# Idle-time products in the routing, a first expert step in two parts, and one leaf for its second block

## The chip, the cores and the metric

The kernel runs on one core of a Trainium2 chip. A core has TensorE (matrix products, written to PSUM), VectorE, ScalarE, GpSimd and SyncE, which run their own instruction streams and wait for each other by semaphores, and 16 DMA engines that move data between HBM and the on-chip memory SBUF. The metric is the device time of one execution in microseconds (us), lower is better; times of a kernel are given as the median of several runs.

## The reference

A decoder trunk of two layers over 256 tokens of 1024 numbers, in float32. Each layer: a mixer (gated MLP over chunks, differential attention, pooling), residual and layer norm, a feed-forward part, residual and layer norm. The feed-forward part of layer 0 is a dense SwiGLU; that of layer 1 sends each token to its two best of eight experts:

```python
logits = (xt @ router_w).astype(F32)
top_v, top_i = lax.top_k(logits, TOP_K)
top_w = jax.nn.softmax(top_v, axis=-1)
gates = jnp.sum(jax.nn.one_hot(top_i, N_EXPERTS, dtype=F32) * top_w[..., None], axis=1)
for e in range(N_EXPERTS):
    y = y + gates[:, e:e + 1].astype(x.dtype) * swiglu(xt, w1[e], w3[e], w2[e])
```

An expert has w1 and w3 of 1024 x 3584 and w2 of 3584 x 1024, so the eight of them are 352 MB, nearly all that the kernel reads.

## The kernel before

Layer 0, the second mixer and the routing come first; the experts take the last two thirds of the time.

**The weights' pieces.** All large weights are cut into pieces of 128 partitions x 1024 numbers (512 KB). The list `units` has them in the order of use, and `pump_loads` (L170) issues a piece's load on SyncE's queue as soon as a place is free. In the expert stage there are 34 places (10 + 8 + 16), and the piece m can be loaded when piece m - 34 has been given back: `place_of` (L155) compares with `state["done"]`, which `done(n)` raises. Places are given back in program order, and a load whose place was read within a branch waits until TensorE has passed that branch. Before the routing has ended, only the pieces whose address is known without it can be loaded; they fill the 34 places.

**The steps.** Each expert is worked through in seven steps of 512 of its 3584 columns. `order()` (L50) interleaves two lanes of experts into 56 steps; steps 0 to 5 and 7 belong to the expert in front of lane 1, called `first`, step 6 to the first one of lane 0. A step takes 4 pieces of w1, 4 of w3 and, but for an expert's first step, 4 of w2 (for the columns of the step before); its program is `step(mode)` in the loop at L1257: `h_part` (L1214) makes the products with w1 into `bank[0]` and with w3 into `bank[1]`, `y_part` (L1243) those with w2, and `turn` (L1225) transposes the result for the next step. After the step `done` gives its pieces back.

**Counts, blocks and leaves.** Which tokens an expert gets is known on the chip alone. `first` is always the weights' expert 0, whatever its count; the other seven are ranked by their count, and `MOST_OF` (L59) says how many tokens the expert of a rank can have at most: 256 for the ranks 0 to 2, 170 for rank 3, 128 and less behind it. Those above 128 have a second block of 128 tokens. `by_count` (L1157) writes each block's work several times, as leaves of an If: "full" for more than 64 tokens in the block, "pair" for 33 to 64 (two groups of 64 columns side by side), "quad" for up to 32 (four of 32). The second block's leaves stand within an If on a count over 128. All leaves are in the instruction stream, one behind another, and an engine jumps over those that are not taken; TensorE's are by far the longest, since each float32 product is two records with a weight load each.

**The routing.** `finish` (L872) is the end of the second mixer for the second 128 tokens: it normalises them, turns them (`turned`, L797), makes their logits (8 products with 8 columns) and chooses two experts per token (`choose`, L814). From `finish` on the instructions of every engine stand in the order in which they are written (`manual_schedule`). Then come the tokens' places within their expert (`pk`, L896 to L899), VectorE's copies of these, the clearing of the PSUM banks that the expert stage uses (L981), the selection matrix of the first expert (`gather_sel`, L1006), the count into registers (`load_count`, L987), the sort of the experts by count, and the gather of the first expert's tokens (`gather`, L1050), 16 products with a moving side of 64 columns. GpSimd scatters the tokens to HBM for the others.

## Time and profile before

| what | value |
|---|---|
| median of 3 runs | 1405.44 us (1399.57 to 1407.64) |
| the profiled execution | 1409.62 us, span 1407.9 us |
| TensorE busy (matmul) | 1254.7 us, 89% |
| VectorE, ScalarE, GpSimd busy | 412.7, 300.8, 103.0 us |
| mean granted clock of TensorE | 0.952 |
| DMA, mean over the span | 316 GB/s |

The span is the time from the program's first instruction to its last; the execution's own time is a little longer. [...] "Busy" of TensorE means that a product is under way. In rows of the timeline a bracket says how long the engine was idle before the row and what ended that; PEq or ACTq is the sequencer of TensorE or ScalarE, which jumps and issues, and "issue" means that nothing in the profile ended the wait.

### The profile page before, as it was taken

The page shows a single profiled execution, that of the slowest core. Times are in us where ns is not written, and L with a number is a line of the kernel's source. Part 1 is how long each engine was busy: PE and PEld are TensorE (multiplying, and loading weights), DVE is VectorE, ACT ScalarE, POOL GpSimd, SP SyncE. Part 2 cuts the span into 40 slices and gives each one's busy share as a digit, 9 for nine tenths or more (in the row PEclk, how much of TensorE's full clock was granted, in tenths as well). Part 3 has the DMA queues.
Part 4 walks back from the last instruction along what each step waited for, and adds up shares of the span by engine and source line. Part 5 has one row for each costly group of instructions (what it writes and reads, how often), then busy time and mean ns, then how long its engine had stood idle before and what let it go on. Part 6 is the DMA issues. An engine that isn't in the chain of part 4 may idle for free. (4 is left out here: it accounts for less than half of the span.)

```text
span 1407.9 us, 18436 instructions
## 1 busy us (share of the span) xinstructions
PE 1254.7 (89%) x6282; PEld 689.6 (49%) x6282; DVE 412.7 (29%) x674; ACT 300.8 (21%) x515; POOL 103.0 (7%) x162
## 2 busy tenths in 40 slices
PE   7989999999888778899989887988988999999875
PEld 6977888879863223334333332423433344433221
DVE  3757454566641111112121111111121021111123
ACT  3646444445520001110011000111110100001101
POOL 2111000010122000000000000000000000000161
PEclk9999999999987989999999999999999999999997
DMA  8995565564495997989999999799999999999995
GB/s 256 385 334 174 187 208 178 186 194 161 119 358 195 343 382 264 339 313 391 392 385 393 393 364 362 263 340 336 368 381 393 385 392 392 393 394 359 397 394 207
DMA packets 204428, 445.38 MB, mean 316 GB/s; under 512 B 14759, under 2 KB 36838, under 8 KB 204232
## 3 DMA queue, kind: packets, MB, share of 16 engines
q1 hardware_dynamic: 199192, 426.49, 83.2%
q0 software_dynamic: 5040, 16.20, 3.2%
q8 instruction: 133, 2.18, 0.6%
q14 instruction: 63, 0.52, 0.1%
HBM read 427.42 MB, written 15.21 MB: 314 GB/s over the span
## 5 line engine op out<-in xcount | busy, mean ns | idle before, releaser
L1182 PE MATMUL bank<-raw,xg 128*32 128x512 f32 (+2 forms) x2240 | 519.4, 639 | 82.9 <-issue 41.7
L1182 PEld LDWEIGHTS bank<-raw,xg 128*32 128x32 f32 (+2 forms) x2240 | 183.7, 141 | 374.1 <-issue 321.2
L1182 PE MATMUL py<-raw,gT 128*64 128x512 f32 (+2 forms) x880 | 226.0, 607 | 3.0 <-issue 1.4
L1223 DVE COPY hB<-bank 128x512 f32<-128x512 f32 x56 | 38.7, 692 | 462.1 <-PE bank L1182 434.6
L199 DVE TENSOR_TENSOR lo<-raw,hi 128x1024 fp32r<-128x1024 f32 x118 | 141.6, 1221 | 85.8 <-ACT hi L198 82.8
L1182 PEld LDWEIGHTS py<-raw,gT 128*64 128x64 f32 (+2 forms) x880 | 85.5, 144 | 132.0 <-issue 115.1
L198 ACT ACTIVATE hi<-raw 128x1024 fp32r<-128x1024 f32 x118 | 121.6, 1056 | 82.2 <-PE h L232 36.2
L1219 ACT ACTIVATE g<-bank 128x512 f32<-128x512 f32 x70 | 41.8, 597 | 339.7 <-PE bank L1182 339.7
L1237 DVE TENSOR_REDUCE gm<-bank 128x128 f32<-128x512 f32 (+1 forms) x112 | 74.1, 688 | 103.5 <-PE bank L1230 99.0
L1240 ACT ACTIVATE gm<-gm 128x128 f32<-128x128 f32 (+1 forms) x56 | 19.6, 350 | 318.1 <-DVE gm L1237 318.1
L232 PE MATMUL h<-hi,x1Th 128*128 128x512 f32 (+1 forms) x192 | 70.8, 375 | 0.8 <-DVE x1Tl L236 0.6
L1221 DVE TENSOR_TENSOR gm<-g,bank 128x512 f32<-128x512 f32 x14 | 9.6, 688 | 208.7 <-PE bank L1182 208.7
L232 PE MATMUL h<-hi,x1Tl 128*128 128x512 f32 (+1 forms) x192 | 70.4, 372 | 0.0
L232 PE MATMUL h<-lo,x1Th 128*128 128x512 f32 (+1 forms) x192 | 54.4, 372 | 0.0
L1037 POOL DMA_DIRECT2D stage<-far_rows x9 | 4.9, 540 | 594.0 <-PE bank L1063 427.5
L1230 PEld LDWEIGHTS bank<-ident,g 128*128 128x128 f32 x224 | 23.8, 142 | 48.4 <-issue 45.0
L1232 ACT ACTIVATE gT<-bank 128x512 f32<-128x512 f32 x14 | 8.4, 597 | 178.7 <-PE bank L1230 178.7
L232 PE MATMUL ph<-hi,mix 128*128 128x512 f32 x128 | 41.0, 397 | 0.0
L232 PEld LDWEIGHTS h<-hi,x1Th 128*128 128x128 f32 x192 | 36.1, 188 | 7.5 <-DVE x1Tl L236 1.0
L232 PEld LDWEIGHTS h<-hi,x1Tl 128*128 128x128 f32 x192 | 36.2, 188 | 6.5 <-DVE x1Tl L236 0.4
L1230 PE MATMUL bank<-ident,hB 128*128 128x128 f32 x224 | 34.9, 279 | 4.5 <-DVE hB L1223 2.3
L1230 PE MATMUL bank<-ident,g 128*128 128x128 f32 x224 | 36.9, 288 | 1.2
(335 smaller groups left out, 1233.3 us busy)
## 6 DMA issues: line engine op xcount, KB each, us to landing
raw<-in_moe_w_dram SPq DMA_DIRECT2D x672, 512.0 KB, 10.5
raw<-in_ffn_w_dram SPq DMA_DIRECT2D x66, 512.0 KB, 4.5
raw<-in_w_in_dram SPq DMA_DIRECT2D x36, 512.0 KB, 4.3
far_rows<-zeros SPq DMA_DIRECT2D x8, 1024.0 KB, 11.7
raw<-in_w_out_dram SPq DMA_DIRECT2D x16, 512.0 KB, 8.8
stage<-far_rows POOLq DMA_DIRECT2D x7, 256.0 KB, 7.8
lnp<-in_ln_g_dram POOLq DMA_DIRECT2D x6, 256.0 KB, 3.7
lnp<-in_ln_b_dram POOLq DMA_DIRECT2D x6, 256.0 KB, 5.6
```

Source lines behind the costliest of these rows:

```text
L198: A.activation(hi, t, AF.Copy)
L199: V.tensor_tensor(lo, t, f32(hi), op=ALU.subtract)
L232: T.matmul(o, st, mv, start=start and i == 0, stop=stop and i == len(pairs) - 1)
L1037: G.dma_start(out=stage[b_][0:w, :], in_=far_rows[r:r + w, :])
L1182: T.matmul(o[j * w:(j + 1) * w], x_(k, w), row[:, cols], start=first and k < parts, stop=last and k >= len(ws) - parts)
L1219: A.activation(gs[b_], o, AF.Silu if mode == "full" else AF.Copy)
L1221: V.tensor_tensor(gm, gs[b_], o, op=ALU.mult)
L1223: V.tensor_copy(hB[b_], o)
L1230: T.transpose(pt[:, c * P:(c + 1) * P], h[:, c * P:(c + 1) * P], ident)
L1232: A.activation(d, bank[2], AF.Copy)
L1237: V.tensor_reduce(t[:, 0:4 * w].rearrange("p (c t) -> p c t", c=4), pt.rearrange("p (c j t) -> p c t j", c=4, j=parts), axis=AX.X, op=ALU.add)
L1240: A.activation(t1, t1, AF.Silu)
```

## The change

There are three edits.

First, `keep_going` makes two products of the identity with rows of `xcur` into a PSUM tile that nobody reads. It is called in `finish` between the row scale and the turning of the tokens, once behind the mixer, and once behind the places `pk`. Its tile comes from the rotation of four banks from which the expert stage takes its own, so one of those is the same memory.

Second, the first expert's second block has one leaf, "full", in the gather and in `by_count`; a leaf for 128 tokens is right for fewer too.

Third, in step 0 the products with w1 are made for all blocks in a `by_count` of their own, the four pieces of w1 are given back, and then the step goes on with w3; `h_part` skips a weight with no pieces.

```diff
@@ finish
         row_scale(xs, nmu, sq, rs)
+        idle.append(rot("idle"))
+        keep_going()
         pl, lg = logits(turned(us))
...
-    lgs, lranks = [], []
+    lgs, lranks, idle = [], [], []
+
+    def keep_going():
+
+        for i in range(2):
+            T.matmul(idle[0], ident, xcur[:, 0, i * 512:(i + 1) * 512], start=True, stop=True)
+
     bias_logits()
     mixer(1, xT, lambda: transpose_x(xT, 1, 0, 8), route_0, bcast(ln1_g[1]), bcast(ln1_b[1]), finish)
+    keep_going()
     pk = acc("pslot")
...
+    keep_going()
     first = LANES[1][0]
@@ gather
-        if MOST_OF[e] > P:
+        if e == first:
+            with tc.If(n > P):
+                block(1, P)
+        elif MOST_OF[e] > P:
@@ by_count
-        if b_:
+        if b_ and e == first:
+
+            with tc.If(n > P):
+                go("full")
+        elif b_:
             with tc.If(n > P):
                 modes()
@@ h_part
         for o, ws in zip(bank, (w1, w3)):
+            if not ws:
+                continue
@@ the loop over the steps
         w2 = take(4) if i else []
+        if s == 0:
+
+            for b_ in blocks(e):
+                by_count(e, b_, lambda mode: h_part(q, b_, mode, w1, []))
+            w1 = []
+            done(4)
...
-        done(8 + len(w2))
+        done(len(w1) + 4 + len(w2))
```

## Rows read from the trace of the kernel before

**Rows 1.** Stretches: length, busy us (instructions) by engine, clock, DMA share, GB/s.
```profile
420.00:442.00 22.00, 17.92 (x72) 10.82 (x72) 5.04 (x19) 2.88 (x6) 9.27 (x26) 0.70 0.24 94
442.00:640.00 198.00, 164.04 (x733) 67.86 (x734) 28.50 (x47) 19.03 (x38) 3.27 (x6) 0.92 0.92 331
640.00:820.00 180.00, 164.49 (x756) 66.72 (x755) 30.29 (x50) 16.59 (x33) 2.17 (x4) 0.96 1.04 391
820.00:1030.00 210.00, 185.62 (x887) 73.65 (x889) 34.30 (x57) 23.34 (x47) 4.29 (x8) 0.95 0.92 337
```

**Rows 2.** Waits over the span: us in total, times, longest.
```profile
PE bank L1182 <- issue: 41.7, 18, 6.9
...
PEld bank L1182 <- DMA raw<-in_moe_w_dram: 32.4, 45, 4.4
...
PE bank L1182 <- PEq L1171: 23.8, 10, 3.8
```

**Rows 3.** Timeline of SyncE's queue from 440 us: start, us, instruction, count.
```profile
442.41 4.00 SPq L184 DMA_DIRECT2D raw<-in_moe_w_dram  x6
```

**Rows 4.** TensorE's timeline, first records of steps 1 to 6 and the gather.
```profile
443.00 8.78 PE L1182 MATMUL bank<-raw,xg 128*64 128x512 f32 x32 [3.68 <-PEq L1171]
...
461.28 8.42 PE L1182 MATMUL bank<-raw,xg 128*64 128x512 f32 x32 [5.04 <-issue]
...
477.49 8.78 PE L1182 MATMUL bank<-raw,xg 128*64 128x512 f32 x32 [3.34 <-PEq L1171]
...
494.58 8.78 PE L1182 MATMUL bank<-raw,xg 128*64 128x512 f32 x32 [3.84 <-PEq L1171]
...
514.75 8.99 PE L1182 MATMUL bank<-raw,xg 128*64 128x512 f32 x32 [6.92 <-issue]
...
531.37 2.14 PE L1063 MATMUL bank<-ident,stage 128*128 128x128 f32 x16 [3.18 <-PEq L1171]
533.44 16.79 PE L1182 MATMUL bank<-raw,xg 128*128 128x512 f32 x32
```

**Rows 5.** TensorE's timeline, later steps without a long gap in front.
```profile
557.82 7.09 PE L1182 MATMUL bank<-raw,xg 128*64 128x512 f32 x32 [0.31 <-ACT gm L1240]
...
570.79 0.93 PE L1063 MATMUL bank<-ident,stage 64*128 64x64 f32 x8 [1.42 <-ACTq L1171]
...
586.89 13.97 PE L1182 MATMUL bank<-raw,xg 128*128 128x512 f32 x32 [0.48 <-PEq L1171]
...
1206.86 7.09 PE L1182 MATMUL bank<-raw,xg 128*64 128x512 f32 x32
```

**Rows 6.** TensorE's timeline, steps behind steps of the expert of rank 3.
```profile
801.77 14.00 PE L1182 MATMUL bank<-raw,xg 128*128 128x512 f32 x32 [0.90 <-ACTq L1171]
...
863.72 8.58 PE L1182 MATMUL bank<-raw,xg 128*64 128x512 f32 x32 [5.20 <-issue]
...
879.80 15.67 PE L1182 MATMUL bank<-raw,xg 128*128 128x512 f32 x32 [3.03 <-PEq L1171]
```

**Rows 7.** Stretches of the routing and one step end; clock third from the right.
```profile
404.00:412.00 8.00, 5.79 (x37) 4.62 (x36) 4.46 (x19) 4.19 (x8) 0.67 (x2) 1.00 1.05 387
413.00:433.00 20.00, 15.01 (x58) 11.43 (x60) 6.51 (x38) 2.55 (x5) 12.85 (x46) 0.50 0.48 185
...
568.00:572.00 4.00, 2.54 (x20) 1.71 (x20) 1.71 (x3) 1.05 (x3) 0.00 (x0) 1.00 0.30 93
```

**Rows 8.** Timeline of all engines in the routing.
```profile
410.66 1.36 PE L803 MATMUL pxT<-ident,u 128*128 128x128 f32 x8 [2.10 <-DVE u L882]
...
411.97 2.86 PE L810 MATMUL plog<-rw,x1T 128*128 128x8 f32 x16
...
418.43 0.66 DVE L1018 TENSOR_SCALAR se<-misc,slot 128x256 f32<-128x256 f32 x2
```

**Rows 9.** TensorE's timeline, the first gather and step 0.
```profile
420.24 7.06 PE L1061 MATMUL bank<-se,xcur 128*128 128x64 f32 x32 [2.45 <-DVE hB L921]
428.10 9.64 PE L1182 MATMUL bank<-raw,xg 128*64 128x512 f32 x32 [0.80 <-POOL hB L947]
```

## The prediction

> **What bounds the kernel now.** I read the stretches first [rows 1]. Where the transfers never wait (640 to 820 us) their share is 1.04, so in another stretch they idle for its length times (1 - share/1.04): 16.9 us of 420 to 442, 22.8 us of 442 to 640, 24.2 us of 820 to 1030. The reader sees a kernel that moves expert weights as fast as it ever does for long stretches, and two places in which the transfers stand still. Then the waits [rows 2]: TensorE waits 32.4 us in all, at 45 places, for weights that have not landed, but at the same line 41.7 and 23.8 us, at 28 places, for nothing that the profile shows or for its own sequencer at a branch. So in the idle stretches it is TensorE that is late: a piece of weights can be loaded only when an earlier one is given back. The queue shows it at the start: the first expert load after the routing leaves at 442.41 [rows 3], 3.1 us after step 0 has ended (its end is 443.00 - 3.68 = 439.32, [rows 4]). What TensorE gains before 640 us the transfers can follow while they have idle time to give, 16.9 + 22.8 = 39.7 us; everything behind then moves forward as a whole.

> **1. The gaps between the steps of the first expert.** Its count picks the middle leaf (64 weight columns, 32 records). In front of steps 1 to 5 and of the next gather TensorE stands 3.68, 5.04, 3.34, 3.84, 6.92 and 3.18 us, 26.0 us in six gaps [rows 4]. In such a gap the sequencer jumps over five leaves: the quad leaf of its own block, three of the second block, the full leaf of the next step. A step of an expert with one block jumps over two, and starts without any idle time (1206.86, [rows 5]). With one leaf in the second block the jump is over three. A straight line between two leaves (0 us) and five (26.0/6 = 4.33 us) gives 1.44 us for three, so six gaps cost 8.7 us and 17.3 us go. The nearest single rows are gaps of 1.42 and 0.90 us, both ended by ScalarE's sequencer [rows 5, 6]: that wait, for the other engines to pass the same branch, is late next and stays. Bounds: if each gap stays as the four that are nearest to each other (3.68, 3.34, 3.84, 3.18: mean 3.51), 5.0 us go; if they vanish, 26.0.

> [...]

> **2. The clock behind those gaps.** [...] A mean of 1.44 us is what four short gaps and two long ones make. Three steps and the full one: 3 x 1.69 + 2.82 = 7.9 us. Bounds 0 and 5 x 1.69 + 2.82 = 11.3.

> **3. The unused products in the routing.** Each call adds two products, four records of 128x512; a record at the high clock takes 13.97/32 = 0.437 us [rows 5], so a call takes 1.75 us, 3.5 us at the low one. The first call fits into the 2.10 us in which TensorE waits for the turned rows (410.66, [rows 8]); the second into the wait for the choice between the logits and the counts (from 411.97 + 2.86 = 414.83; the gather starts at 420.24); without that cover it costs its 1.75 us. The third stands between the counts and the gather. Today the clock is 1.00 up to 412 and 0.50 from 413 to 433 [rows 7]. Held high, the gather of 7.06 us is halved (3.5 us), the logits' 2.86 us lose some 0.7, and step 0's 9.64 us become the 7.09 us of 557.82 (2.55 us) [rows 5, 8, 9]. Between the last unused product and step 0 lies the gather with its 64-column products, during 7.06 us of which the clock does not rise now; whether it falls during 3.5 us no row shows, so I count half of the 2.55: 3.5 + 0.7 + 1.3 = 5.5 us. Bounds: 6.8 us, and -3.5 us if the clock falls all the same and the third call then stands in front of the gather at the low clock.

> A wait is added: the bank of the unused products is cleared by VectorE before it is reused, so this clearing waits for the third call, and behind it on VectorE stand the selection for the gather, the sort and all that follows. The selection ends at 418.43 + 0.66 = 419.09, 1.15 us before the gather starts [rows 8, 9]; the third call ends some 1.1 us after the clearing would have run. The 1.15 us hide it. Without that cover it costs 1.1 us. SyncE's registers and GpSimd's places come later by as much, and neither is needed before the next expert.

> **4. Step 0 in two parts.** TensorE does the same products; it passes one more pair of branches, over leaves of 16 records. I take 0; the bounds are 0, since nothing is removed there, and a loss of one long gap, 3.5 us. The queue gets its first four pieces after the w1 products instead of after both: gather from about 419.5, 3.5 us long, the 0.80 us of [rows 9], then half of 7.09 us: 427.4 instead of 442.41. By itself this is worth nothing to TensorE, which lacks no weights there; it is what lets the transfers follow (they give back 15 of the 28.7 us here). SyncE has nothing else in line behind these loads. GpSimd's four scatters now share the engines with them.

> **5. Code behind the first expert.** It moves forward by the leaves removed, so jumps fall differently on what is fetched. The expert of rank 3, also with two blocks, has five such gaps, 0.90 us in one and 3.03 to 5.20 in the others, of which three stand in the rows [rows 6]; the short one may become long: I take a loss of 2.0 us, between a gain of 5 (two long gaps that lose a second fetch, 2.5 us each as under E) and a loss of 8.4 (two places at 4.2). Step 7 and the last w2 part have a short gap (1.42) already: 0.

> **Sum.** 17.3 + 7.9 + 5.5 - 2.0 = 28.7 us. The profiled execution took 1409.62 us (span 1407.9 us and 1.7 us around it), 4.2 us above the median of 1405.44. Taken off it: 1380.9 us; taken off the median, which is what is predicted: 1376.7, so 1377 us.

> **The rivals.**
> A, the forecast: chance 0.58. Its own range is 1366 to 1386.
> B, the shorter jump is still too long: each gap keeps one fetch (3.51 us), the clock still falls behind it. 5.0 + 5.5 us go: 1395 us. For it: four of the six gaps are nearly equal though they begin at different places, as if one fetch were due whatever the length. Against it: jumps over two leaves cost nothing. Chance 0.16.
> C, the transfers become the bound: only the earlier restart counts, 15 us, and the idle time from 442 to 640 is eaten by scatters, reads and partly filled releases: 1390 us. Against it: TensorE lacks weights almost nowhere, so a fuller or emptier store of pieces is not felt at once. Chance 0.08.
> D, the clock falls in the routing all the same: 28.7 - 5.5 = 23.2 us, or less by 3.5: 1382 to 1386 us. Chance 0.07.
> E, slower: the code behind falls worse on the fetches. Without the five of the first expert's steps, 23 of the 28 places of [rows 2] remain, with 42.7 us. A second fetch in a gap costs (5.04 + 6.92)/2 - 3.51 = 2.5 us, and 1.69 us of clock: 4.2 us a place. From seven places on the 28.7 us are gone; with nine it is 1405.4 + 9.1 = 1414.5 us. Against it: some places must also get better. Chance 0.06.
> The remaining 0.05 is for B and part of E together, about the time of before.

> **How the numbers follow.** 0.5% is 7 us, about what a measurement here can tell from no change. A, B, C and D lie beyond it on the fast side (0.89, less 0.03 for the upper edge of B): 0.86. Slower: E, 0.06. Within: 0.08. The range goes from 1362 (the upper bounds of parts 1 to 3: 26.0 + 11.3 + 6.8 = 44.1 us, 1361.3) to 1397 (B with the 2.0 us of part 5), and leaves out E and the rest.

> **What would show it.** Right: in front of steps 1 to 5 and the gather two or three idle times over 3 us instead of six; the first expert load near 427 us; granted clock 1.00 from 412 to 419 and a gather of about 3.5 us; the first full step beginning some 25 us earlier than 533.44; transfers idle some 11 us instead of 39.7 before it has caught up. Wrong: six gaps of about 3.5 us (B); TensorE waiting for weights from 560 us on (C); the gather at 7 us (D); more and longer sequencer waits from 560 us on (E).

## The result: 1392.7 us beside 1401.7, and the profile after

The changed kernel takes 1392.74 us (median of 6 runs, 1390.43 to 1398.24), the kernel before 1401.70 in 6 runs (1399.57 to 1407.64). The ratio is 0.9932, with a 95% interval from 0.9904 to 0.9959: 9 us less, between 6 and 13. The forecast was 1377 us and a gain of 28.7. The profiled execution took 1393.96 us, 15.7 less than the one before. That is 6.7 us more than between the medians: the profiled execution of before was 7.9 us above its median, the one after 1.2 us. What the traces show as gained and lost below belongs to these two executions; where the 6.7 us lie no run here shows.

The mechanisms in front came true, and in the traces about half of what they gained was lost again behind them. First the routing and the first expert, TensorE's timeline of the kernel after (start, length, instruction, in brackets the idle time in front and what ended it), to be read against [rows 4, 8, 9]:

```profile
412.07 1.96 PE L900 MATMUL idle<-xcur,ident 128*128 128x512 f32 x4
...
418.46 3.76 PE L1071 MATMUL bank<-se,xcur 128*128 128x64 f32 x32 [0.95 <-DMA raw<-in_moe_w_dram]
422.92 3.66 PE L1199 MATMUL bank<-raw,xg 128*64 128x512 f32 x16 [0.70 <-POOL place L836]
427.15 3.65 PE L1199 MATMUL bank<-raw,xg 128*64 128x512 f32 x16 [0.58 <-PEq L1185]
...
433.08 7.09 PE L1199 MATMUL bank<-raw,xg 128*64 128x512 f32 x32 [0.69 <-ACTq L1185]
...
445.52 7.09 PE L1199 MATMUL bank<-raw,xg 128*64 128x512 f32 x32 [0.90 <-ACTq L1185]
...
460.08 7.09 PE L1199 MATMUL bank<-raw,xg 128*64 128x512 f32 x32 [3.01 <-DMA raw<-in_moe_w_dram]
...
475.14 8.78 PE L1199 MATMUL bank<-raw,xg 128*64 128x512 f32 x32 [3.52 <-issue]
...
489.40 7.09 PE L1199 MATMUL bank<-raw,xg 128*64 128x512 f32 x32 [1.02 <-ACTq L1185]
...
501.84 0.66 PE L1073 MATMUL bank<-ident,stage 128*128 128x128 f32 x4 [0.90 <-ACTq L1185]
...
504.32 13.97 PE L1199 MATMUL bank<-raw,xg 128*128 128x512 f32 x32
```

The gather takes 3.76 us instead of 7.06, two long gaps are left of six, and the first full step starts at 504.32 instead of 533.44, 29.1 us earlier.

Then the stretches of [rows 1], after the change (columns as there, the DMA share is the last but one):

```profile
420.00:442.00 22.00, 19.66 (x102) 9.08 (x103) 5.11 (x17) 2.71 (x7) 7.37 (x24) 1.00 0.65 235
442.00:640.00 198.00, 174.70 (x854) 70.94 (x850) 34.52 (x57) 21.36 (x43) 5.17 (x8) 0.97 1.00 369
640.00:820.00 180.00, 155.01 (x692) 61.46 (x694) 27.33 (x45) 15.68 (x31) 2.17 (x4) 0.92 0.98 365
820.00:1030.00 210.00, 181.27 (x870) 70.29 (x870) 33.17 (x56) 22.74 (x46) 4.29 (x8) 0.93 0.91 333
```

With length x (1 - share/1.04) the transfers idle 8.3 + 7.6 us up to 640 instead of 39.7: 23.8 won. From 640 to 1030 they idle 10.4 + 26.3 = 36.7 us instead of 24.2: 12.5 lost. The same can be followed more finely by asking, in both traces, when a given amount of weights was still to come (worked out from the packets of the weights' queue; the last 1 MB on it is the result):

```
MB still to come   before, us   after, us   lead of the transfers, us
     336             419.9        418.5        1.5
     296             566.7        545.0       21.7
     280             621.3        593.1       28.2
     212             798.9        770.6       28.3
     200             831.1        813.2       17.8
     184             874.9        861.0       13.8
     172             920.7        900.6       20.1
     152             983.8        972.4       11.4
     136            1028.1       1013.3       14.9
      72            1193.9       1179.4       14.5
       0            1404.9       1389.3       15.7
```

The lead reaches 28.3 us, near the 30.7 us that parts 1 to 3 of the forecast sum to, and stays there for 177 us in which the transfers never wait; 1.5 us of it were there at 420 us, before the first expert began. It is lost between 770 and 980 us and does not come back, because the transfers hardly pause behind that (share 1.04 from 1015 to 1290 us). TensorE's own lead does grow again, to 29.9 us at 1301, but it buys nothing: in the last 80 us TensorE waits 12.4 us for weights, and the end comes when the last of them do. The waits of the w2 products over the span, of before and after (us, times, longest):

```profile
PE py L1182 <- DMA raw<-in_moe_w_dram: 1.2, 6, 0.2
```
```profile
PE py L1199 <- DMA raw<-in_moe_w_dram: 8.7, 14, 1.7
```

Where it is lost the trace shows at once. The rows of before at those places, first; [rows 6] has two of them:

```profile
740.64 3.49 PE L1097 MATMUL bank<-yt,misc 128*32 128x512 f32 x4 [1.85 <-ACT yt L1093]
...
787.63 8.78 PE L1182 MATMUL bank<-raw,xg 128*64 128x512 f32 x32 [3.56 <-PEq L1171]
...
845.28 8.78 PE L1182 MATMUL bank<-raw,xg 128*64 128x512 f32 x32 [3.70 <-PEq L1171]
```

And the kernel after, the same products:

```profile
715.05 3.44 PE L1110 MATMUL bank<-yt,misc 128*32 128x512 f32 x4 [6.55 <-PEq L1188]
...
767.63 9.65 PE L1199 MATMUL bank<-raw,xg 128*64 128x512 f32 x32 [8.79 <-DMA raw<-in_moe_w_dram]
784.64 13.97 PE L1199 MATMUL bank<-raw,xg 128*128 128x512 f32 x32 [2.91 <-PEq L1188]
...
827.92 1.08 PE L1199 MATMUL bank<-raw,xg 128*64 128x512 f32 x1 [3.35 <-PEq L1188]
830.67 8.42 PE L1199 MATMUL bank<-raw,xg 128*64 128x512 f32 x30 [1.66 <-issue]
847.43 8.78 PE L1199 MATMUL bank<-raw,xg 128*64 128x512 f32 x32 [3.46 <-PEq L1188]
861.72 14.00 PE L1199 MATMUL bank<-raw,xg 128*128 128x512 f32 x32 [1.05 <-ACTq L1188]
```

Of this code the change altered next to nothing (9 more semaphore instructions behind the product at 767.63), only where it lies. TensorE's program of 34,125 instructions is 1,684 shorter now, and the records of the trace can be counted off against the instructions of the program. The page shows how it is brought in, before and after (packets, MB, share of 16 engines):

```profile
q8 instruction: 133, 2.18, 0.6%
```
```profile
q8 instruction: 126, 2.06, 0.6%
```

That is 16.4 KB a packet (every one of the 133 and 126 has 16,384 bytes). The two programs, 34,125 and 32,441 instructions, make 256.6 and 257.5 a packet, so about 256 instructions of 64 bytes as an estimate, and as many packets as the whole program is long: leaves that are jumped over are loaded too. The arrival of such a packet is what the forecast calls a fetch. Where one packet ends and the next begins the waits in mid-leaf show: of the 37 waits over 1.25 us between 440 and 1060 us, in all ten kernels, that have no jump in front, 36 stand within two instructions of the same place modulo 256 (here 525.34 and 640.70 are two of them, at 193 and 194). While TensorE stands in front of the product at 767.63 (from 758.84 us), two packets arrive (the stretch 758 to 769 of the DMA view), and only one in the same wait of before, 784.07 to 787.63 (the stretch 778 to 789):

```profile
q8 instruction: 2, 0.03, 1.2%
```
```profile
q8 instruction: 1, 0.02, 0.6%
```

The jump is 568 instructions long in both kernels. Before it starts 112 instructions into a packet and crosses two boundaries, now at 211 and crosses three. The fold at 715.05 (the products that add up the column groups of a finished expert's result) stands behind a jump of 340, which crossed one boundary and now crosses two. So theory 1: the place of the later code relative to the packets gives the loss. Theory 2, forecast rival C in another form: the transfers limit, and whatever TensorE gains in front is eaten behind. The rows of the timeline alone don't decide between them: the longest wait is put down to "DMA raw", which may mean weights. The packets of the instruction queue say more, counted off in order: all 14 waits over 1.6 us between 440 and 1060 us of the changed kernel end 1.3 to 2.4 us after the landing of the very packet that holds the next instruction, that at 767.63 1.7 us after it. In all ten kernels of this study 119 of 122 such waits do. So these waits are for code; what they cost in time the experiments have to show.

### The profile page after: what moved, and what is told of

The parts are those of the page before. It is cut to its first block, busy times and chain, and to the rows that moved or that the text cites. A ratio compares the mean times of both kernels' runs of the same rounds, so it can differ in the third digit from the quotient of the medians.

```text
span 1392.3 us, 18479 instructions
## 1 busy us (share of the span) xinstructions
PE 1251.2 (90%) x6294; PEld 676.7 (49%) x6294; DVE 414.3 (30%) x674; ACT 300.5 (22%) x515; POOL 102.8 (7%) x162
## 5 line engine op out<-in xcount | busy, mean ns | idle before, releaser
L1199 PE MATMUL bank<-raw,xg 128*32 128x512 f32 (+2 forms) x2240 | 505.9, 626 | 66.1 <-issue 25.4
L1199 PEld LDWEIGHTS bank<-raw,xg 128*32 128x32 f32 (+2 forms) x2240 | 175.8, 139 | 356.7 <-issue 308.9
L1199 PE MATMUL py<-raw,gT 128*64 128x512 f32 (+2 forms) x880 | 233.6, 618 | 10.4 <-DMA raw<-in_moe_w_dram 8.1
L1249 PEld LDWEIGHTS bank<-ident,g 128*128 128x128 f32 x224 | 23.5, 140 | 48.0 <-issue 43.8
L232 PEld LDWEIGHTS h<-lo,x1Th 128*128 128x128 f32 x192 | 34.5, 188 | 6.3
```

What stands on the lines that cost most here:

```text
L232: T.matmul(o, st, mv, start=start and i == 0, stop=stop and i == len(pairs) - 1)
L1199: T.matmul(o[j * w:(j + 1) * w], x_(k, w), row[:, cols], start=first and k < parts, stop=last and k >= len(ws) - parts)
L1249: T.transpose(pt[:, c * P:(c + 1) * P], h[:, c * P:(c + 1) * P], ident)
```

## The experiments

Each was timed beside the kernel before: e1 to e4 beside 1404.39 us, e5 to e8 beside 1401.62. Products that never run stand in leaves that the counts do not pick (a product is four TensorE instructions here). The places were matched by the length of the whole program; counted at single jumps, the code behind the first expert lies up to 10 instructions off the place named in e1, e4 and e5.

**Run e1: the later code back at its old offsets.**

```diff
             if b_:
+                if e == first and i == nb - 1 and hf == 0:
+                    for _ in range(37):
+                        T.matmul(o, ident, w2[0][:, 0, 0:512], start=True, stop=True)
                 d = y1[q][:, hf]
```

> The changed kernel with 37 products that never run (148 TensorE instructions) in the leaf of the first expert's second block that its count does not pick, behind its last step. They move all later TensorE code back to the same offset, modulo 256 instructions, that it has in the kernel before. Theory 1 (the place of the code): the weights' transfers lead by 28.3 us at 770 us and by 14.6 at 1013 us because the jumps behind the first expert now cross more 16 KB packets of instructions that are not yet there. With the offsets of before, the waits of TensorE from 600 us on are those of before (the 6.55 us in front of the fold near 715 back to about 1.9, the 8.79 near 768 to about 3.6), the 13.7 us come back, and the time is 1379 us (1375 to 1383). Theory 2 (the transfers): what TensorE gains in front is lost behind 770 us because the weights cannot come faster, wherever the code lies: 1392.7 us, within 3.

Measured: 1384.43 us, ratio 0.9861 (0.9835 to 0.9888). The two places:

```profile
717.01 1.90 PE L1110 MATMUL bank<-yt,misc 128*32 128x512 f32 x4 [1.69 <-ACT yt L1106]
762.17 9.86 PE L1199 MATMUL bank<-raw,xg 128*64 128x512 f32 x32 [3.51 <-PEq L1188]
```

Both waits are those of before (1.85 and 3.56). By the packets the transfers lead by 24.1 us from 1010 us to the end instead of 14.6. Nothing but code that never runs was added, and the kernel became 8 us faster (10 by the ratios): theory 2 falls. It is 5 us short of the 1379 and just outside the range given; shifting cost something too: the lead at 720 us is 22.2 and not 28.3 (waits of 2.6, 1.9 and 4.5 us between 554 and 604 that the changed kernel does not have).

**Run e2: a whole packet, the same offsets.** As e1, with 64 products.

> The same with 64 products that never run, 256 instructions: the offsets modulo 256 stay those of the changed kernel, and one jump is longer by a whole packet. Theory 1: the changed kernel's time, 1392.7 us, or up to 3.5 us more for the one longer jump; the waits near 715 and 768 us stay at about 6.6 and 8.8. If any shift of the code helped by itself, this one would also be at 1379. Theory 2: 1392.7.

Measured: 1400.87 us, ratio 0.9978 (0.9956 to 1.0001).

```profile
555.42 6.17 PE L1199 MATMUL bank<-raw,xg 128*32 128x512 f32 x32 [5.64 <-issue]
...
721.60 3.27 PE L1110 MATMUL bank<-yt,misc 128*32 128x512 f32 x4 [6.62 <-PEq L1188]
...
773.77 9.68 PE L1199 MATMUL bank<-raw,xg 128*64 128x512 f32 x32 [8.79 <-DMA raw<-in_moe_w_dram]
```

The waits near 715 and 768 stayed to 0.1 us, as theory 1 says. The longer jump cost more than the 3.5 us allowed: 5.64 us instead of 1.04, and its 32 records took 6.17 us where quad leaves at a granted clock of 1.00, which is full speed, take 3.64 (580.64 in the changed kernel), 7.1 us together. So a shift does not help as such; this one cost 8 us by the medians, 6 by the ratios, whose intervals just touch.

**Run e5: the same in the kernel before.** Its edit is that of e1, with 27 products and `mode == "full"` in the condition, in the kernel before.

> The kernel before, with nothing of the change, and 27 products that never run (108 TensorE instructions) in an unused leaf behind the first expert's last step: all later code then has the offsets modulo 256 that it has in the changed kernel. Theory 1 (the place of the code): from 600 us on TensorE waits where the changed kernel waits (about 6.5 us in front of the fold near 741, 8.8 near 790), the transfers lose 10 to 14 us against the kernel before, and the time is 1416 us (1411 to 1420) beside 1404. Theory 2 (the loss in the changed kernel comes from its own lead, the transfers being the limit): products that never run cost nothing, 1404 within 3.

Measured: 1421.34 us beside 1401.62, ratio 1.0133 (1.0106 to 1.0160): slower by 20 us, by code that never runs; the direction is theory 1's, the size more than the 12 us that it gave.

```profile
744.74 3.59 PE L1097 MATMUL bank<-yt,misc 128*32 128x512 f32 x4 [6.58 <-PEq L1171]
...
797.93 8.54 PE L1182 MATMUL bank<-raw,xg 128*64 128x512 f32 x32 [8.75 <-DMA raw<-in_moe_w_dram]
814.12 15.67 PE L1182 MATMUL bank<-raw,xg 128*128 128x512 f32 x32 [3.19 <-PEq L1171]
```

The waits are the changed kernel's (6.55, 8.79, 2.91), though this kernel has no lead that the transfers could take back; TensorE is 10 us later here than in the kernel before. So the 8.79 us were no wait for weights, whatever the row names. The transfers lose 16 us by 1060 us. One place is worse than in the changed kernel: near 862 us a jump starts 9 instructions later than there, crosses three boundaries instead of two and waits 6.47 us.

**Run e4: without the unused products.**

```diff
         for i in range(2):
-            T.matmul(idle[0], ident, xcur[:, 0, i * 512:(i + 1) * 512], start=True, stop=True)
+            pass
...
             with tc.If(n > P):
+                for i in range(9):
+                    T.matmul(bank[2], ident, xcur[:, 0, (i % 2) * 512:(i % 2 + 1) * 512], start=True, stop=True)
                 block(1, P)
```

> The changed kernel without the six unused products of the routing; nine products that never run stand in the unused leaf of the first gather, so that the code behind lies where it does in the changed kernel (1 instruction off). The forecast's term for them was 5.5 us: the gather near 420 us takes about 7 us again instead of 3.76, step 0 some 9.6 instead of 7.3, the first expert's step 1 begins 5 to 7 us later. Theory 1: this difference stays to the end, 1398 us (1396 to 1400). Theory 2: the transfers swallow it, 1392.7.

Measured: 1399.80 us, ratio 0.9961 (0.9940 to 0.9983); the gather takes 7.06 us again, step 0 6.40 and 3.65 instead of 3.66 and 3.65, and step 1 starts at 437.59 instead of 433.08: 4.5 us. This execution was 1.5 us ahead when the tokens' turning began (407.42 against 408.95); counted from there the products are worth 6.0 us, close to the term of 5.5. By the ratios the whole kernel gains 0.29%, 4 us, with intervals that overlap; the medians, from two sittings, give 7. Neither is a clean price: the code of the first expert lies 13 instructions off the changed kernel's here, and the jump near 464 crosses one boundary and waits 0.91 us instead of 3.01.

**Run e6: step 0 whole.** The block `if s == 0` is left out, and two products that never run stand in the unused leaf of the first gather.

> The changed kernel with the first expert's step 0 whole again (2 products that never run keep the code behind within 2 instructions of its place). By the forecast's part 4 TensorE does the same, and the weights' queue starts again some 7 us later than 426.69 us. Theory 1: the transfers stand still for about 7.6 us between 442 and 600 us in the changed kernel (158 us at a share of 0.99 against 1.04), which can take up that start: 1392.7 us, up to 4 more. Rival: each us of later start stays, about 1400 us.

Measured: 1396.80 us (1391.27 to 1401.08), ratio 0.9951 (0.9930 to 0.9972), which overlaps the changed kernel's. The first load starts at 430.60 instead of 426.69, 3.9 us later (5.0 counted from the gather's start) and not 7, and the lead of the transfers still reaches 31 us at 620: the later start is taken up. The rival's 1400 is not met. Against that one wait appeared (5.70 us near 688, in front of a leaf that lies 2 instructions off) and another shrank (5.87 us near 770 instead of 8.79, over the same three boundaries), so the value of the split, 3 to 4 us by these times, is not settled.

**Run e3: expert 3, the expert of rank 3, with one leaf as well.**

```diff
-        if b_ and e == first:
+        if b_ and e in ONE:
```

with `ONE = (first, 3)`, and the same in the gather.

> The changed kernel with one leaf for the second block of expert 3 (rank 3) as well, in its steps and its gather. Theory 1: the waits in front of expert 3's steps and the gather behind them (8.79, 2.91, 3.35 and 1.66, 3.46, 1.05 us between 767 and 862) go to about 1 us each, some 15 us, of which the transfers can use what they lose there now, 28.3 - 13.8 = 14.5 us; the code behind expert 3 moves by another 1,684 instructions (148 modulo 256) and falls anew, which I cannot size better than a loss of up to 9 us as in the changed kernel behind 900 us: 1378 us, between 1372 and 1390. Theory 2: 1392.7, within 3.

Measured: 1358.85 us, ratio 0.9670 (0.9645 to 0.9694).

```profile
749.81 7.09 PE L1200 MATMUL bank<-raw,xg 128*64 128x512 f32 x32 [0.91 <-ACTq L1186]
762.25 14.00 PE L1200 MATMUL bank<-raw,xg 128*128 128x512 f32 x32 [0.90 <-ACTq L1186]
...
803.06 7.09 PE L1200 MATMUL bank<-raw,xg 128*64 128x512 f32 x32 [1.01 <-ACTq L1186]
817.46 8.78 PE L1200 MATMUL bank<-raw,xg 128*64 128x512 f32 x32 [2.86 <-issue]
831.60 14.00 PE L1200 MATMUL bank<-raw,xg 128*128 128x512 f32 x32 [0.90 <-ACTq L1186]
```

34 us less than the changed kernel, twice and more what I expected. I had counted only what the changed kernel loses at expert 3 against the kernel before; but the kernel before idles there too (24.2 us from 820 to 1030, [rows 1]), and the fold in front (6.55 us) waited for the same skipped leaves: its jump is 176 instructions now, its wait 1.41. The transfers lead by 48 us at 880.

**Runs e7 and e8: e3 moved by 8 and by 40 instructions.**

```diff
             with tc.If(n > P):
+                for i in range(2 if e == first else 0):
+                    T.matmul(bank[2], ident, xcur[:, 0, (i % 2) * 512:(i % 2 + 1) * 512], start=True, stop=True)
                 block(1, P)
```

> The version with one leaf for expert 3 (run e3) and 2 products that never run (8 instructions) in the unused leaf of the first gather, so that all code from the first expert on lies 8 instructions further. Theory 1: a jump of 335 instructions crosses two packet boundaries where it starts at offset 177 or more; with 8 more, the jumps from 253 (first expert, 2.78 us near 457) and from 252 (expert 3, 2.86 us near 817) start at the head of the next packet and cross one: both waits go to about 1 us, 4 to 5 us in all with the clock behind the first, of which the transfers' idle time (6 us before 600, 8 us from 880 to 1000) decides how much shows: 1355 us (1350 to 1359). Theory 2: 1358.9.

> The same with 10 products that never run (40 instructions). Theory 1: the same two jumps cross one boundary, and the jumps near 936 and 979 us, which start 61 and 52 instructions into a packet and find the next one not yet there (4.52 and 5.89 us), start 40 instructions later, which at 0.06 us each takes some 2 us off each; against it the quad leaf near 523 us reaches the end of its packet 2 us earlier: 1352 us (1346 to 1360). Theory 2: 1358.9.

Measured: e7 1353.62 us (1353.16 to 1355.33), ratio 0.9653 (0.9628 to 0.9678), the lowest median of this study, though by the ratios only 2 us below e3 with intervals that overlap; e8 1358.49 us, 0.9690 (0.9664 to 0.9715). In e7 both jumps cross one boundary, and their waits are gone as expected:

```profile
458.67 7.09 PE L1202 MATMUL bank<-raw,xg 128*64 128x512 f32 x32 [0.91 <-ACTq L1188]
...
815.65 7.09 PE L1202 MATMUL bank<-raw,xg 128*64 128x512 f32 x32 [0.91 <-ACTq L1188]
```

In e8 they are gone as well (0.89 near 462, 0.90 near 818), but the 1352 were missed. New is a wait in a running leaf that reaches the end of its packet before the next one is there (436.19); and the wait near 525, in the changed kernel 3.94 us in mid-leaf, now stands behind a jump over two boundaries and is longer:

```profile
436.19 7.43 PE L1202 MATMUL bank<-raw,xg 128*64 128x512 f32 x25 [3.21 <-issue]
...
524.84 5.87 PE L1202 MATMUL bank<-raw,xg 128*32 128x512 f32 x32 [5.55 <-issue]
```

Counting boundaries in the jumps is half of theory 1, then. The other half, how long after entering a packet the next one is there, could not be foreseen from the rows to better than a few us: in the changed kernel, between 440 and 1060 us, it landed 4.35 us after the first record of the packet in front at the median of 70, and 1.6 to 5.1 us after it in eight of ten.

## Why the prediction was wrong

Its mechanisms held in front, where the transfers led by 28.3 us and parts 1 to 3 sum to 30.7; one term, part 5, was mis-sized, and it decides the time. The gain fell short by 19.7 us (28.7 forecast, 9.0 between the medians). Part 5 is 11.4 of it, as the profiled executions show; that these two are 6.7 us further apart than the medians is most of the rest, and its cause stays open. The forecast's base of 1405.44 us, the median of three runs, was itself 3.7 us above that of six, which made the miss in time smaller.

- **Part 1, the gaps (17.3):** six gaps of 10.0 us in all are left (0.69, 0.90, 3.01, 3.52, 1.02, 0.90), so 16.0 went. They are four short ones and two long, as assumed. The straight line between two leaves and five was the wrong reason, and that its sum came out is luck: a jump over three leaves (335 instructions) crosses two boundaries (3.01 and 3.52 us) or one (about 1 us) by where it starts.
- **Part 2, the clock (7.9):** four of five steps take 7.09 us at a granted clock of 1.00, the one behind the longest gap 8.78 at 0.81; 43.8 us [rows 4] became 37.1. The full step takes 13.97 (1.00) instead of 16.79 (0.83). Together 9.4. The term's 1.69 us are the 8.78 of 443.00 (0.81) less the 7.09 of 557.82 (1.00), its 2.82 us the 16.79 of 533.44 less the 13.97 of 586.89 [rows 4, 5]. That a short gap leaves the clock up rested on one row, 1.42 us at 570.79 with 1.00 from 568 to 572 [rows 5, 7]; now steps behind 0.69, 0.90, 1.02 and even 3.01 us ran at 1.00.
- **Part 3, the unused products (5.5):** the granted clock is 1.00 from 413 to 433 us, where it was 0.50 [rows 7]; run e4 gives 4.5 us at step 1, 6.0 counted from the turning of the tokens. The price named for VectorE's clearing was there and was hidden, as forecast: the clearing at 417.59 waited 0.92 us for the third call, and the gather still starts 9.5 us behind the turning of the tokens (9.6 before, 9.4 in e4). That it starts 1.8 us earlier than before is no gain of the change: the turning began 1.7 us earlier in this execution.
- **Part 4, step 0 in two parts (0):** the second part starts 0.58 us behind the first; the first load left at 426.69, forecast 427.4. Right within what e6 can tell.
- **Part 5, the code behind (-2.0, bounds -5 to +8.4):** this failed. By the transfers the code behind lost 28.3 - 14.9 = 13.4 us in these two executions. Four things were wrong in it. It looked at the gaps of expert 3 alone, and the fold in front (+4.7 us) was not among them. It took a second fetch at 2.5 us, an estimate from the gaps of [rows 4], and 1.69 us of clock; the jump that now crosses three boundaries lost 5.2 us of waiting and 0.9 of clock (9.65 us at 0.73 against 8.78 at 0.81). And it netted gains against losses, though they fall at different times: 863.72 and 879.80 did get better by 1.7 and 2.0 us, after the transfers had already stood still for the pieces that came back late. The short gap that "may become long" did (801.77: 0.90 us, now 784.64: 2.91). And it counted nothing behind expert 3, where waits grew too (0.98 us at 933.04 before, 2.93 at 915.16 now).
- **The rivals:** E named the mechanism, at a chance of 0.06; it came with about half of the 28.7 us that would have undone everything. C named the place where a loss becomes final, but e1 and e5 show that the transfers did not cause it. That the measured 1392.7 lies next to C's 1390 and B's 1395 is chance: TensorE's waits moved the time, and B's six gaps did not stay.

Its offsets could have been had beforehand: the instructions between two records can be counted, the shift at the jump in front of 767.63 is 1,693 instructions, 157 modulo 256, and a jump whose start moves from 112 to 211 in its packet gains a boundary.

How the wait goes with the boundaries was counted between 440 and 1060 us. In the ten kernels 161 of 171 jumps over one boundary wait less than 1.9 us. The other ten waited 3.6 to 5.9 us; all ten start 28 to 76 instructions into a packet, when the next one had not landed yet (it landed 1.3 to 1.7 us before the end of the wait). Those over two boundaries wait 2.4 to 4.0 us at 15 of 29 places in the kernels before and after, 5.0 to 6.6 at three and 1.4 or less at the other eleven, and up to 6.7 in the ten kernels; those over three 5.9 to 8.8. A jump is not needed for it: in the run of e8 a leaf stood 3.21 us in mid-course, with no jump in front of that record, when it came to the end of its packet.

## What to carry to other kernels

Where an engine's program is long and full of leaves that are not taken, its length and its offset are part of every change (run e5: 20 us for 108 instructions that never run): count the packets that each jump crosses before and after, also in code that the edit does not touch. Fewer leaves are worth more than their rare use suggests (run e3: 34 us for two conditions), and a few instructions that never run are a cheap way to test whether a time depends on placement at all (runs e1 and e5). Where transfers are the limit over long stretches, follow the transfers' lead and not the engine's: what is gained in front of a stretch in which they idle anyway stays only if that stretch does not get worse (here a lead of 28.3 us became 14.9).
